# Attention of a hybrid block: order of the tensor engine's work within a unit

## The chip, the cores and the metric

The kernel runs on one core of a Trainium2 chip, one launch for both layers. The metric is the time of one execution on the device in microseconds (us), the median of three runs. A profile shows one execution, with every instruction of the engines: TensorE (PE, its weight loads PEld), VectorE (DVE), ScalarE (ACT), GpSimd (POOL) and the queue of SyncE that issues DMAs (SP).

## What is computed

Two layers over 512 latent tokens and 256 context tokens of width 1024. Each layer projects its input once and feeds three branches (attention, a state space scan, a convolution module); each branch is projected again, multiplied by a gate and summed. What matters here is the attention and the gated sum:

```python
def _attend(q, k, v):
    s = jnp.einsum('bkgqd,bksd->bkgqs', q, k).astype(jnp.float32) * ATTN_SCALE
    p = jax.nn.softmax(s, axis=-1).astype(v.dtype)
    return jnp.einsum('bkgqs,bksd->bkgqd', p, v)

def gated_merge(ua, us, uc, gm, w_br_attn, w_br_ssd, w_br_conv, b_gate, w_out):
    g = jax.nn.sigmoid(gm.reshape(gm.shape[:-1] + (N_BRANCH, D_MODEL)) + b_gate)
    y = (g[..., 0, :] * (ua @ w_br_attn) + g[..., 1, :] * (us @ w_br_ssd)
         + g[..., 2, :] * (uc @ w_br_conv))
    return y @ w_out
```

There are 8 query heads on 2 key heads, of width 64. Latent queries read all 768 keys, context queries the 256 context keys. The second layer computes no context queries.

## The kernel before

Large projections (`mm_cm_steps`, L175) are sums of three matmuls of split operands: `hh`/`hl` are the high and low parts of the input, `whi`/`wlo` those of a weight, which arrives by DMA as `raw` and is split by ACT (L156) and DVE (L157). A step yields after at least 1,024 columns of matmul, so that such work can be handed out in small portions.

Attention goes in **units**: one pair of heads `hp2` (4 pairs) by one block of 128 queries `qi`. The first layer has 24 units (16 of latent queries, 8 of context queries), the second 16, all latent. Between `man.__enter__()` and `man.__exit__()` the order of PE's instructions is the order of the code; the other engines' order is chosen at build time by a scheduler with a timing model, by priority and readiness (weight loads have high priority), and is fixed in the program. Each engine runs its own list strictly in order and waits on semaphores.

A latent unit consists of these parts:

- `scores` (tiles `ps_l`, two banks of 512 columns, and `ps_c`, one bank for both heads' 256 context keys): 4 + 4 matmuls; DVE takes three maxima (L988, L992) and joins them (L995). The banks come from the pool `pw`, which has three.
- `exps`, a generator: ACT reads the three banks with four exponentials and their sums (L1004, L1006), DVE inverts the sums (L1010), and ACT (L1012) and DVE (L1014) scale one head's `pe` each.
- `turn`, three times: four transposes of `pe` by PE into a bank `pt_p`, copied into `pth` by ACT (L1034) or, the second one, by DVE (L1032).
- `pv`: 24 matmuls of `pth` with the values into a bank `po_v`, each of 64 columns of the array, two side by side; ACT copies the result into `oa` (L1050).

`pt_p` and `po_v` share the pool `po1` of three banks with `pt_qk` (transposes of rotated queries and keys, run by `pipe.turn()`) and `ps_mod` (the next layer's modulation, first layer only). A bank is handed on when its last reader is done. `pth` tiles come from a pool of seven small tiles.

A context unit has one bank of scores, one `turn` and 8 value matmuls.

Between these parts the merge of the scan's branch is handed out: `wv = Weave(...)` runs the gate projection `ps_gm` (24 matmuls per 512 columns of output), the branch projection `ps_br` (12) and, in the first layer, `ps_mod`. Its total of columns is divided by a count of turns: 13 (`ATTN_SPARE`, 9 in the second layer) plus 8 for each latent unit and 7 for each context unit. `wv.fill(w)` hands out w turns' worth; `wv.finish()` hands out what is left. So a turn, here called a piece, is 247,808 / 197 = 1,258 columns in the first layer and 159,744 / 137 = 1,166 in the second.

The code runs the units in a pipeline of depth one: for unit u, first `scores` of unit u + 1, with a piece after each of its three banks; then u's three `turn`s, each followed by one step of u + 1's exponentials and a piece; a piece; u's values; a piece. After a pair's last unit, `oa` is multiplied by the gate (L1077) and stored (L1079). Behind the units, `ua` (high and low part of each pair's output) is built from `oa` by ACT (L1089) and DVE (L1090), and the attention branch's merge reads it (`ps_br<-ua`).

Of the kernel before, what the change touches and what calls it, by code (L numbers as in the profile page):

```python
# [9 lines left out]
F32 = mybir.dt.float32  # L10
F32R = mybir.dt.float32r
AF = mybir.ActivationFunctionType
ALU = mybir.AluOpType
AX = mybir.AxisListType

P = 128
# [5 lines left out]
NTT = NT // P  # L22
NLT = NL // P
# [24 lines left out]
ATTN_SPARE = (13, 9)  # L48
CTX_TURN = 1.75
# [8 lines left out]
def hybrid_kernel(ctx, tc, xT, cc, consts, rope, mod_params, params, fnw, w_mod, w_cm, w_q, w_kvd, w_z,  # L58
                  w_br, w_out, out):
    nc = tc.nc  # L60
    V, S, G, T = nc.vector, nc.scalar, nc.gpsimd, nc.tensor
# [5 lines left out]
    mid = ctx.enter_context(tc.tile_pool(name="mid", bufs=1))  # L67
    wk = ctx.enter_context(tc.tile_pool(name="wk", bufs=6))
    fl = ctx.enter_context(tc.tile_pool(name="fl", bufs=3))
# [16 lines left out]
    def fill(shape, name):  # L86
        return fl.tile(shape, F32, tag="F", name=name)
# [7 lines left out]
    def pot(name):  # L95
        return po1.tile([P, 512], F32, tag="po1", name=name)
# [7 lines left out]
    def tok(tt):  # L104
        return slice(tt * P, (tt + 1) * P)
# [77 lines left out]
    def run(steps):  # L183
        for _ in steps:
            pass
# [122 lines left out]
    o_dr = [dr.tile([P, NT], F32, name=f"odr{k}") for k in range(4)]  # L308
# [3 lines left out]
    ga_dr = [dr.tile([P, NT], F32, name=f"gadr{k}") for k in range(4)]  # L312
# [4 lines left out]
    for li in range(2):  # L317
# [3 lines left out]
        ntok = NL if last else NT  # L321
        ntt = ntok // P
# [3 lines left out]
        def rope_tables(cw, sw, o, eng):  # L326
# [5 lines left out]
            for hf in range(2):  # L332
                for b in range(2):
# [9 lines left out]
                        op0=ALU.mult)  # L343
# [18 lines left out]
        for k in range(0, KD, 2):  # L362
            if li == 0:
                for q in (4 + k // 2, k // 2):
                    wm = bigt([P, 2, KD, P], F32, "wm")
                    with tc.high_priority(offset=2 * TOP):
# [4 lines left out]
                                   in1=pmod[:, li, O_NW + k:O_NW + k + 2].unsqueeze(2).to_broadcast([P, 2, 2]),  # L371
                                   op0=ALU.add, op1=ALU.mult)
# [540 lines left out]
        for j in range(len(decays) + ahead):  # L913
            i = j // 2
# [54 lines left out]
        qts.append(bigt([P, 4, ntok], F32R, "qt"))  # L969
        later = [partial(q_prep, 1, t0) for t0 in range(0, ntt, 2)]  # L970

        def scores(hp2, qi, fill):

            g, hq = hp2 // 2, hp2 % 2 * 2
            lat = qi < NLT
            pl = [pwt("ps_l") for _ in range(2)] if lat else []
            pc2 = pwt("ps_c")
            mx = sm.tile([P, 2, 2], F32, tag="mx", name="mx", bufs=4)

            def qk(ps, j, a, b):  # L980
                for i in range(2):
                    T.matmul(ps[:, 0:b - a], qts[g][:, hq + j, tok(qi)], kk[:, i, g, a:b], start=(i == 0),  # L982
                             stop=(i == 1))

            if lat:
                for j in range(2):
                    qk(pl[j], j, 0, 512)
                    V.tensor_reduce(out=mx[:, 0, j:j + 1], in_=pl[j], axis=AX.X, op=ALU.max, negate=True)  # L988
                    fill()
            for j in range(2):  # L990
                qk(pc2[:, j * 256:(j + 1) * 256], j, 512, 768)
            V.tensor_reduce(out=mx[:, 1, :], in_=pc2.rearrange("p (j k) -> p j k", j=2), axis=AX.X, op=ALU.max,  # L992
                            negate=True)
            if lat:
                V.tensor_tensor(out=mx[:, 1, :], in0=mx[:, 0, :], in1=mx[:, 1, :], op=ALU.min)  # L995
            fill()
            sr = sm.tile([P, 2, 2], F32, tag="sr", name="sr", bufs=4)
            pes = [work([P, (NTT if lat else 2) * P], F32, "pe") for _ in range(2)]

            def exps():  # L1000
                for j in range(2):
                    bias, r = mx[:, 1, j:j + 1], sr[:, 1, j:j + 1]
                    if lat:
                        S.activation(pes[j][:, 0:512], pl[j], AF.Exp, bias=bias, accum_out=sr[:, 0, j:j + 1])  # L1004
                        yield
                    S.activation(pes[j][:, 512 if lat else 0:], pc2[:, j * 256:(j + 1) * 256], AF.Exp, bias=bias,  # L1006
                                 accum_out=r)
                    if lat:
                        V.tensor_tensor(out=r, in0=sr[:, 0, j:j + 1], in1=r, op=ALU.add)
                    V.reciprocal(r, r)  # L1010
                    if j == 0:
                        S.activation(pes[j], pes[j], AF.Copy, scale=r)  # L1012
                    else:
                        V.tensor_scalar(out=pes[j], in0=pes[j], scalar1=r, scalar2=None, op0=ALU.mult)  # L1014
                    yield

            return pes, exps()

        def values(hp2, qi, pes, oa, nexp, fill):
            g = hp2 // 2  # L1020
            k0, nk = (0, NTT) if qi < NLT else (NLT, NTT - NLT)
            po = pot("po_v")

            def turn(k1):
                pt = pot("pt_p")
                for i in range(2):
                    for j in range(2):
                        T.transpose(pt[:, tok(2 * i + j)], pes[j][:, tok(k1 + i)], ident)  # L1028
                pth = small([P, 2, 2, P], F32, "pth")
                pf = pth.rearrange("p k j q -> p (k j q)")  # L1030
                if k1 == 2:
                    V.tensor_copy(pf, pt)  # L1032
                else:
                    S.activation(pf, pt, AF.Copy)  # L1034
                next(nexp, None)
                fill()
                return pth

            def pv(k1, pth):
                for i in range(2):  # L1040
                    for j in range(2):
                        T.matmul(po[64 * j:64 * j + 64, 0:P], vv[:, k0 + k1 + i, g, :], pth[:, i, j, :],  # L1042
                                 start=(k1 + i == 0), stop=(k1 + i == nk - 1), tile_position=(0, 64 * j))

            pths = [turn(k1) for k1 in range(0, nk, 2)]
            run(nexp)
            fill()
            for k1, pth in zip(range(0, nk, 2), pths):
                pv(k1, pth)
            S.activation(oa[:, tok(qi)], po[:, 0:P], AF.Copy)  # L1050
            fill()


        units = [(hp2, qi) for hp2 in range(HEADS // 2) for qi in range(ntt)]
        while pipe.done < NTT // 2 + 1:
# [4 lines left out]
        wv = Weave(chain(merge_steps(1, us, False, False), ahead_steps(ahead0, ahead1)),  # L1060
                   merge_cols + (ahead1 - ahead0) * 24 * ntok,
                   ATTN_SPARE[li] + sum(8 if qi < NLT else 4 * CTX_TURN for _, qi in units))
        pes, exps = scores(*units[0], wv.fill)
        run(exps)
        for ui, (hp2, qi) in enumerate(units):
            cur = pes
            exps = iter(())
            pipe.turn()
            if ui + 1 < len(units):
                pes, exps = scores(*units[ui + 1], wv.fill)  # L1070
            if qi == 0:
                oa = mid.tile([P, ntok], F32, tag="H", name="oa", bufs=2)
            values(hp2, qi, cur, oa, exps, wv.fill if qi < NLT else partial(wv.fill, CTX_TURN))
            if qi == ntt - 1:
                gl = fl.tile([P, ntok], F32, tag="C", name="gl", bufs=1)
                nc.sync.dma_start(gl, ga_dr[hp2][:, :ntok])
                V.scalar_tensor_tensor(out=oa, in0=oa, scalar=0.5, in1=gl, op0=ALU.mult, op1=ALU.mult)  # L1077
                if hp2 < 3:
                    nc.sync.dma_start(o_dr[hp2][:, :ntok], oa)  # L1079
        wv.finish()  # L1080
        man.__exit__(None, None, None)

# [179 lines left out]
```

## Time and profile before

| | |
|---|---|
| median of 3 runs | 1495.2 us (1494.25 to 1498.19) |
| profiled execution: time of the run | 1495.54 us |
| profiled execution: span, first to last instruction | 1493.8 us |
| mean granted TensorE clock | 0.994 |
| attention of layer 1, from the first scores | about 520 to 718 us |
| attention of layer 2, from the first scores | about 1239 to 1383 us |

The page of a profile gives each engine's busy time and its share of the span; the rows below come from it and from views of the trace: sums over stretches of time ("windows"), who waited for whom ("waits"), and the instructions in order of time ("timeline"). Two neighbouring matmuls overlap in the records, since they are pipelined: the distance between their starts, not their duration, is what one costs.

### The profile page before, as it was taken

How to read it: one execution, taken by the hardware profiler on the slowest of the kernel's cores; microseconds unless marked ns; L12 is line 12 of the kernel's file. 1: busy time of each engine (PE TensorE's matmuls, PEld its weight loads, DVE VectorE, ACT ScalarE, POOL GpSimd, SP SyncE). 2: the span in 40 equal slices, each digit the busy share in tenths (PEclk: the TensorE clock that was granted, in tenths of full speed). 3: DMA queues.
4: the chain of work that ended last, by engine and by line, in shares of the span. 5: the costliest groups of instructions: out<-in, count | busy, mean ns of one | idle time of the engine just before them, and what ended most of it. 6: DMA issues, size and time to landing. Idle time of an engine off the chain costs nothing.

```text
span 1493.8 us, 25061 instructions
## 1 busy us (share of the span) xinstructions
PE 1450.1 (97%) x9716; PEld 1255.5 (84%) x9716; DVE 1039.1 (70%) x1911; ACT 721.9 (48%) x1624; POOL 81.6 (5%) x177
## 2 busy tenths in 40 slices
PE   5999999999999999999999989999999999999997
PEld 4889899988888888888888877989988887888886
DVE  4689998666568675555344377899977788666564
ACT  4423543364445475555333154355455557666341
POOL 0000010100002110000000000001010021000000
PEclk9999999999999999999999999999999999999998
DMA  9222333223233322323652532213423242322542
GB/s 377 69 72 94 108 117 111 76 71 103 100 114 123 124 94 99 121 64 121 226 176 92 173 114 86 82 57 110 152 78 106 96 151 78 105 85 91 185 141 78
DMA packets 69687, 172.58 MB, mean 116 GB/s; under 512 B 7872, under 2 KB 24384, under 8 KB 69568
## 3 DMA queue, kind: packets, MB, share of 16 engines
q1 hardware_dynamic: 69568, 170.98, 34.8%
q8 instruction: 76, 1.25, 0.3%
q14 instruction: 43, 0.35, 0.1%
HBM read 143.43 MB, written 27.53 MB: 114 GB/s over the span
## 4 chain that ended last, share of the span: by engine, by line
PE 91%; DMA 2%; DVE 2%; ACT 2%; issue 1%; SPq 0%; POOL 0%; POOLq 0%; DVEq 0%; ACTq 0%
PE ps_gm L175 23%; PE ps_br L175 11%; PE ps_xbc L175 9%; PE ps_o L175 6%; PE ps_gcv L175 4%; PE ps_g L175 4%; PE ps_u L175 4%; PE po_v L1042 3%; PE ps_ga L175 3%; PE pt_p L1028 3%; PE ps_l L982 2%; PE ps_mod L229 2%; PE ps_z L216 1%; PE ps_q L216 1%; PE ps_q L217 1%; PE ps_z L217 1%
## 5 line engine op out<-in xcount | busy, mean ns | idle before, releaser
L156 ACT ACTIVATE whi<-raw 128x512 fp32r<-128x512 f32 (+1 forms) x316 | 199.0, 632 | 280.8 <-PE ps_gm L175 63.8
L157 DVE TENSOR_TENSOR wlo<-raw,whi 128x512 fp32r<-128x512 f32 (+1 forms) x316 | 216.9, 690 | 148.0 <-ACT whi L156 144.0
L175 PE MATMUL ps_gm<-hh,whi 128*128 128x512 f32 (+1 forms) x576 | 212.6, 369 | 0.0
L408 DVE SCALAR_TENSOR_TENSOR vacc<-vt,par,vacc 128x783 f32<-128x783 f32 (+1 forms) x232 | 206.5, 890 | 8.1 <-ACT vacc L405 4.5
L175 PE MATMUL ps_gm<-hh,wlo 128*128 128x512 f32 (+1 forms) x576 | 210.1, 365 | 0.0
L175 PE MATMUL ps_gm<-hl,whi 128*128 128x512 f32 (+1 forms) x576 | 209.6, 364 | 0.0
L175 PEld LDWEIGHTS ps_gm<-hh,whi 128*128 128x128 f32 x576 | 109.0, 189 | 16.4 <-issue 3.1
L175 PEld LDWEIGHTS ps_gm<-hh,wlo 128*128 128x128 f32 x576 | 109.0, 189 | 15.1 <-issue 1.7
L175 PEld LDWEIGHTS ps_gm<-hl,whi 128*128 128x128 f32 x576 | 109.0, 189 | 13.8 <-issue 0.9
L175 PE MATMUL ps_xbc<-hh,whi 128*128 128x512 f32 (+1 forms) x240 | 83.0, 346 | 0.0
L175 PE MATMUL ps_xbc<-hh,wlo 128*128 128x512 f32 (+1 forms) x240 | 82.1, 342 | 0.0
L175 PE MATMUL ps_xbc<-hl,whi 128*128 128x512 f32 (+1 forms) x240 | 82.0, 342 | 0.0
L1034 ACT ACTIVATE pth<-pt_p 128x512 f32<-128x512 f32 x72 | 43.6, 605 | 55.8 <-PE pt_p L1028 55.7
L653 ACT ACTIVATE tg<-ps_gm,hw 128x512 f32<-128x512 f32 x72 | 44.2, 614 | 51.1 <-PE ps_gm L175 51.1
L175 PE MATMUL ps_o<-yh,whi 128*128 128x256 f32 (+1 forms) x208 | 65.8, 317 | 1.5 <-DVE xnew L1105 1.4
L175 PE MATMUL ps_o<-yl,whi 128*128 128x256 f32 (+1 forms) x208 | 65.7, 316 | 0.0
L175 PE MATMUL ps_o<-yh,wlo 128*128 128x256 f32 (+1 forms) x208 | 65.7, 316 | 0.0
L522 DVE SCALAR_TENSOR_TENSOR xacc<-xraw,par,xacc 128x770 f32<-128x770 f32 (+1 forms) x64 | 63.4, 999 | 3.0 <-ACT xacc L519 2.8
L682 DVE SCALAR_TENSOR_TENSOR tg<-tg,ps_br 128x512 f32<-128x512 f32 x66 | 39.6, 600 | 34.0 <-PE ps_br L175 30.5
L1028 PE MATMUL pt_p<-mr,pe 128*128 128x128 f32 x416 | 62.4, 272 | 0.0
L988 DVE TENSOR_REDUCE mx<-ps_l 128x1 f32<-128x512 f32 x64 | 44.1, 690 | 24.1 <-PE ps_l L982 23.4
L1028 PEld LDWEIGHTS pt_p<-mr,pe 128*128 128x128 f32 x416 | 50.9, 140 | 11.7 <-issue 0.2
(276 smaller groups left out, 3661.7 us busy)
## 6 DMA issues: line engine op xcount, KB each, us to landing
raw<-in_w_cm_dram SPq DMA_DIRECT2D x96, 512.0 KB, 3.6
raw<-in_w_mod_dram SPq DMA_DIRECT2D x32, 512.0 KB, 3.6
raw<-in_w_br_dram SPq DMA_DIRECT2D x24, 512.0 KB, 3.7
raw<-in_w_out_dram SPq DMA_DIRECT2D x21, 512.0 KB, 3.7
wm<-in_w_mod_dram SPq DMA_DIRECT2D x16, 512.0 KB, 9.2
ydr<-tg SPq DMA_DIRECT2D x16, 384.0 KB, 4.9
yo<-ydr SPq DMA_DIRECT2D x16, 384.0 KB, 3.8
raw<-in_w_z_dram SPq DMA_DIRECT2D x8, 512.0 KB, 3.9
```

The lines of the kernel that those rows point to most:

```text
L156: S.activation(hi, raw[:, u0:u0 + m, :], AF.Copy)
L157: V.tensor_tensor(out=lo, in0=raw[:, u0:u0 + m, :], in1=f(hi), op=ALU.subtract)
L175: T.matmul(ps[:, :b - a], st[:, col], mv(k)[:, a:b], start=(n == 0), stop=(n == len(order) - 1))
L216: T.matmul(ps[:, :ncol], xh(k)[:, t], hi, start=(k == 0), stop=False)
L408: V.scalar_tensor_tensor(out=acc[:, :n] if j else vt[:, o:o + n], in0=vt[:, o + j:o + j + n], scalar=cw(j), in1=acc[:, :n], op0=ALU.mult, ...
L522: xm = V.scalar_tensor_tensor(out=acc[:, :n], in0=raw[:, j:j + n], scalar=par[:, O_SCW + ct * 5 + j:O_SCW + ct * 5 + j + 1], in1=acc[:, :n ...
L653: lambda ps, a, b: S.activation(tg[:, a:b], ps, AF.Tanh, scale=0.5, bias=hw[:, br * 8 + ct:br * 8 + ct + 1]), "ps_gm")
L682: V.scalar_tensor_tensor(out=tg[:, a:b], in0=tg[:, a:b], scalar=1.0, in1=ps, op0=ALU.add, op1=ALU.mult)
L988: V.tensor_reduce(out=mx[:, 0, j:j + 1], in_=pl[j], axis=AX.X, op=ALU.max, negate=True)
L1028: T.transpose(pt[:, tok(2 * i + j)], pes[j][:, tok(k1 + i)], ident)
L1034: S.activation(pf, pt, AF.Copy)
L1042: T.matmul(po[64 * j:64 * j + 64, 0:P], vv[:, k0 + k1 + i, g, :], pth[:, i, j, :], start=(k1 + i == 0), stop=(k1 + i == nk - 1), tile_posi ...
```

## The change

The parts of a unit are put in another order on PE. For unit u: the eight score matmuls of unit u + 1 in one go; six pieces of the merge (a context unit: three of 1.75), after each of them but the last ones a step of the exponentials of u + 1; then, without a piece between, the values of unit u - 1 and all transposes of unit u; then two pieces (a context unit: one of 1.75). So the values run one unit later than before, the copies `pth` live on until then, and the gate of `oa` moves into `values`. Before the loop, the first unit's scores are followed by half of `ATTN_SPARE` in pieces (6.5 and 4.5); the last unit's values run after the loop, followed by what is left of the merge.

```diff
-        def scores(hp2, qi, fill):
+        def scores(hp2, qi):
...
                     V.tensor_reduce(out=mx[:, 0, j:j + 1], in_=pl[j], axis=AX.X, op=ALU.max, negate=True)
-                    fill()
...
                 V.tensor_tensor(out=mx[:, 1, :], in0=mx[:, 0, :], in1=mx[:, 1, :], op=ALU.min)
-            fill()
...
-        def values(hp2, qi, pes, oa, nexp, fill):
-            g = hp2 // 2
-            k0, nk = (0, NTT) if qi < NLT else (NLT, NTT - NLT)
-            po = pot("po_v")
-
-            def turn(k1):
+        def turned(hp2, qi, pes):
+
+            pths = []
+            for k1 in range(0, NTT if qi < NLT else NTT - NLT, 2):
                 pt = pot("pt_p")
...
-                next(nexp, None)
-                fill()
-                return pth
-
-            def pv(k1, pth):
-                for i in range(2):
-                    for j in range(2):
-                        T.matmul(po[64 * j:64 * j + 64, 0:P], vv[:, k0 + k1 + i, g, :], pth[:, i, j, :],
-                                 start=(k1 + i == 0), stop=(k1 + i == nk - 1), tile_position=(0, 64 * j))
-
-            pths = [turn(k1) for k1 in range(0, nk, 2)]
-            run(nexp)
-            fill()
-            for k1, pth in zip(range(0, nk, 2), pths):
-                pv(k1, pth)
+                pths.append(pth)
+            return pths
+
+        def values(hp2, qi, pths):
+            g, k0, nk = hp2 // 2, 0 if qi < NLT else NLT, 2 * len(pths)
+            po = pot("po_v")
+            for k in range(nk):
+                for j in range(2):
+                    T.matmul(po[64 * j:64 * j + 64, 0:P], vv[:, k0 + k, g, :], pths[k // 2][:, k % 2, j, :],
+                             start=(k == 0), stop=(k == nk - 1), tile_position=(0, 64 * j))
+            if qi == 0:
+                oas.append(mid.tile([P, ntok], F32, tag="H", name="oa", bufs=2))
+            oa = oas[-1]
             S.activation(oa[:, tok(qi)], po[:, 0:P], AF.Copy)
-            fill()
+            if qi == ntt - 1:
+                gl = fl.tile([P, ntok], F32, tag="C", name="gl", bufs=1)
+                nc.sync.dma_start(gl, ga_dr[hp2][:, :ntok])
+                V.scalar_tensor_tensor(out=oa, in0=oa, scalar=0.5, in1=gl, op0=ALU.mult, op1=ALU.mult)
+                if hp2 < 3:
+                    nc.sync.dma_start(o_dr[hp2][:, :ntok], oa)
...
-        pes, exps = scores(*units[0], wv.fill)
+        oas, before = [], None
+        pes, exps = scores(*units[0])
+        wv.fill(ATTN_SPARE[li] / 2)
         run(exps)
-        for ui, (hp2, qi) in enumerate(units):
+        for ui, unit in enumerate(units):
             cur = pes
             exps = iter(())
             pipe.turn()
             if ui + 1 < len(units):
-                pes, exps = scores(*units[ui + 1], wv.fill)
...
+                pes, exps = scores(*units[ui + 1])
+            lat = unit[1] < NLT
+            turns = 8 if lat else 4
+            for t in range(turns):
+                if t == turns * 3 // 4:
+                    run(exps)
+                    if before is not None:
+                        values(*before)
+                    before = (*unit, turned(*unit, cur))
+                next(exps, None)
+                wv.fill(1 if lat else CTX_TURN)
+        values(*before)
+        oa = oas[-1]
         wv.finish()
```

## Rows read from the trace of the kernel before

**Rows 1.** The page: busy time, share of the span and instructions of each engine.
```profile
PE 1450.1 (97%) x9716; PEld 1255.5 (84%) x9716; DVE 1039.1 (70%) x1911; ACT 721.9 (48%) x1624; POOL 81.6 (5%) x177
```

**Rows 2.** Windows: both attention stages; engines' busy us (instructions), granted clock, DMA.
```profile
520.00:718.00 198.00, 196.24 (x1593) 165.87 (x1592) 118.03 (x281) 122.25 (x319) 6.19 (x6) 1.00 0.33 106
1238.60:1383.00 144.40, 142.58 (x1022) 115.97 (x1023) 101.48 (x229) 95.27 (x240) 3.66 (x4) 0.99 0.26 86
```

**Rows 3.** Windows, the same columns: one latent unit of layer 2, transposes to transposes.
```profile
1311.39:1319.93 8.54, 8.54 (x63) 6.99 (x62) 7.11 (x16) 5.57 (x14) 0.00 (x0) 1.00 0.42 139
```

**Rows 4.** Waits of PE: line, waited for: us in total, times, longest.
```profile
PE ps_l L982 <- ACT pe L1004: 3.0, 2, 1.5
...
PE po_v L1042 <- ACT pth L1034: 0.2, 1, 0.2
```

**Rows 5.** Timeline at the head of layer 1's attention: start, us, instruction [idle before].
```profile
523.44 0.80 PE L857 MATMUL pt_qk<-mr,qhl 128*128 128x128 f32 x8
...
524.90 0.69 ACT L1004 ACTIVATE pe<-ps_l,mx 128x512 f32<-128x512 f32 x1
...
525.74 0.73 PE L982 MATMUL ps_l<-kk,qt 128*128 128x512 f32 x2 [1.50 <-ACT pe L1004]
```

**Rows 6.** Timeline of PE: transposes, then values, between pieces of the merge.
```profile
1304.65 0.60 PE L1028 MATMUL pt_p<-mr,pe 128*128 128x128 f32 x4
1305.00 0.48 PE L175 MATMUL ps_gm<-hh,wlo 128*128 128x512 f32 x1
1305.32 0.40 PE L175 MATMUL ps_gm<-hh,whi 128*128 128x512 f32 x1
1305.55 0.40 PE L175 MATMUL ps_gm<-hl,whi 128*128 128x512 f32 x1
...
1314.79 0.40 PE L175 MATMUL ps_gm<-hl,whi 128*128 128x512 f32 x1
1315.11 1.53 PE L1042 MATMUL po_v<-pth,vv 128*64 128x128 f32 x24
1316.58 0.50 PE L175 MATMUL ps_gm<-hh,wlo 128*128 128x512 f32 x1
1316.91 0.39 PE L175 MATMUL ps_gm<-hh,whi 128*128 128x512 f32 x1
```

**Rows 7.** Timeline of PE: transposes directly behind narrow matmuls.
```profile
548.50 0.65 PE L229 MATMUL ps_mod<-raw,sc 128*32 128x128 f32 x16
549.07 0.66 PE L1028 MATMUL pt_p<-mr,pe 128*128 128x128 f32 x4
...
549.80 0.39 PE L175 MATMUL ps_gm<-hl,whi 128*128 128x512 f32 x1
```

**Rows 8.** Timeline: ACT's copy of the values' bank, two units with and one without delay.
```profile
554.58 0.26 ACT L1050 ACTIVATE oa<-po_v 128x128 f32<-128x128 f32 x1
...
1316.69 0.28 ACT L1050 ACTIVATE oa<-po_v 128x128 f32<-128x128 f32 x1
...
1374.94 1.53 PE L1042 MATMUL po_v<-pth,vv 128*64 128x128 f32 x24
...
1376.03 0.97 ACT L1012 ACTIVATE pe<-pe,sr 128x768 f32<-128x768 f32 x1
1376.86 0.72 ACT L653 ACTIVATE tg<-ps_gm,hw 128x512 f32<-128x512 f32 x1
1377.43 0.31 ACT L1050 ACTIVATE oa<-po_v 128x128 f32<-128x128 f32 x1
```

**Rows 9.** Timeline behind layer 2's attention: first merge matmul of `ua`, last low part.
```profile
1392.94 0.62 PE L175 MATMUL ps_br<-ua,whi 128*128 128x512 f32 x2
...
1394.83 0.69 DVE L1090 TENSOR_TENSOR ua<-og,ua 128x512 fp32r<-128x512 f32 x1 [0.56 <-ACT ua L1089]
```

**Rows 10.** Windows, columns as in rows 2: a stretch of transposes and waits, and the next.
```profile
1235.90:1239.30 3.40, 2.35 (x18) 1.78 (x18) 2.73 (x7) 3.25 (x7) 1.05 (x1) 1.00 0.63 199
1239.30:1242.70 3.40, 3.40 (x10) 2.63 (x9) 2.31 (x6) 0.72 (x2) 0.00 (x0) 0.50 0.02 6
```

More of the change, by code (lines that the diff above doesn't have):

```diff
@@ L1069, in hybrid_kernel @@
             if ui + 1 < len(units):
-                pes, exps = scores(*units[ui + 1], wv.fill)
[L1071 to L1079, printed above, removed]
+                pes, exps = scores(*units[ui + 1])
[11 more added lines that the diff above has]
+        oa = oas[-1]
         wv.finish()
```

## Prediction

> **What bounds the kernel now.** I read the page first: PE is busy for 97% of the span, every other engine for at most 70% [rows 1]. A busy share alone says little, since matmuls overlap in the records, so the next question is whether PE ever stands still where the change works. The windows over the two attention stages answer it: PE is idle for 1.76 us of 198 and 1.82 us of 144.4 [rows 2], 3.6 us in all. The view of PE's waits names nearly all of that: twice 1.5 us in which the second unit's `ps_l` waits for the first unit's exponentials, and one 0.2 us wait of `po_v` [rows 4]. A latent unit in the middle of a stage has no idle time at all: 8.54 us, PE busy for 8.54 [rows 3]. So reordering can gain by three ways only: the 3.6 us of idle time, a cheaper passage from one kind of matmul to the next, and a higher clock. It can lose wherever a wait that a piece of the merge covers today is laid bare.
>
> **What a unit costs on PE, by starts.** Merge matmuls of 512 columns start every 0.23 us (1305.32, 1305.55) [rows 6]. Four transposes at 1304.65 put off the second matmul behind them to 1305.32: 0.67, less one matmul's 0.23, is 0.44, or 0.11 a transpose. For the values: from the merge matmul at 1314.79 to the second one behind at 1316.91 are 2.12 us, less two matmuls, 1.66; 12 pairs at 0.11 would be 1.32, so going into and out of the narrow matmuls costs 0.34. The transposes show no such price: four single ones cost as much as a run of them would. A piece is 1,166 columns x 0.23 / 512 = 0.52 us in the second layer and 1,258 columns, 0.57 us, in the first.
>
> **The change, part by part.**
>
> *Scores in one go.* Eight matmuls of the same kind as the merge's; splitting them cost nothing, joining them gains nothing. The three banks are needed at once and earlier: the next unit's scores start when the exponentials of the last must have read them. From the end of the scores to the next scores there were five pieces, transposes and values; now there are eight pieces, transposes and values, about 1.5 us more. No wait here inside the stage: 0.
>
> *6.5 or 4.5 pieces behind the first scores.* This is where both 1.5 us waits stand. In layer 1 PE goes from `pt_qk` at 523.44 (8 transposes) into a wait until 525.74, and the first exponential starts at 524.90 [rows 5]. Behind the first unit's last scores there was one piece so far; with 6.5 and 4.5 there are 5.5 and 3.5 more, 3.1 and 1.8 us of matmul in front of the second unit's scores. Both exceed the 1.5 us of wait, the second by little. I take both waits as gone: -3.0, and -0.2 for the values' wait on `pth`, which is now a unit old when it is read. Bounds: -3.2 and, if the waits move to the next bank, -1.5.
>
> *Values and transposes together.* The narrow matmuls are still entered from a merge matmul, but left into transposes. The trace has one neighbour of that: transposes directly behind `ps_mod`, also narrow [rows 7]. `ps_mod` ends at 549.15 (548.50 + 0.65), the second merge matmul behind the four transposes starts at 549.80, 0.65 later; behind `po_v`, ending at 1316.64, the second merge matmul comes at 1316.91, 0.27 later [rows 6]. Four transposes thus cost 0.38 there instead of 0.44: -0.06 a unit, and for 24 + 16 units -2.4. Bounds: 0 (the passage is no cheaper with `po_v`) and -0.17 a unit, half of the 0.34 if the way out cost nothing, -6.8.
>
> *The banks of `po1`.* A latent unit's group takes four banks out of three: `po_v`, then three `pt_p`. Pieces used to lie between; now the third set of transposes needs the bank of `po_v`, copied out by ACT. From rows 7, the first transposes start 0.08 before the end of the narrow ones, the first four take 0.41 (549.07, and a merge matmul that starts behind them), the second four 0.44: the third four are due 0.77 us after the values' end. An undelayed copy ends in time: `po_v` ends at 1316.64, `oa` runs from 1316.69 to 1316.97, 0.33 after [rows 6, 8]. But ACT works in order. In the last but one unit the values end at 1376.47, ACT still has a scaling of 0.97 and a gate of 0.72, and `oa` ends at 1377.74, 1.27 after: 0.50 too late [rows 8]. Of the 32 latent units, 12 have their copy end later than 0.77 after the values (the first starts at 554.58, the last at 1377.43 [rows 8]), and their excess adds up to 4.6 us. Today nothing waits for it. Does the change empty ACT's list in front of the copy? The values come six pieces behind the scores, 3.1 us, instead of five pieces and three sets of transposes, 3.9; the exponentials and the scaling hang on the scores and come no sooner. In that unit the scaling ended at 1377.00, 0.5 behind the values' end, and an earlier group only widens that. I therefore carry the 4.6 over. Bounds: 0, where the scheduler puts the copy first, and 0.5 in each of 32 units, +16.
>
> *Behind the attention.* `wv.finish()` covers 4.5 instead of 9 pieces, 2.4 us less in layer 2, while the chain from `oa` to the last low part of `ua` stays. There that part starts at 1394.83 and takes 0.69, while the merge of `ua` starts at 1392.94 [rows 9]: within the first tiles it comes just in time. The order is the scheduler's again there and it can put gate projections first: +0.5, bounds 0 and +2.4.
>
> *Nothing, or hidden:* the later store of `oa` (its reader comes behind the attention); DVE's three maxima in a row (2.1 us, then pieces of 3 us); six small tiles in place of three at the moment when old and new `pth` meet (of seven; the old three are read before the new ones are written).
>
> **The sum.** -3.0 - 0.2 - 2.4 + 4.6 + 0.5 = -0.5. The profiled execution took 1495.5 us with what lies around its span, 0.3 above the median; the forecast is 1495.0, no change. A measurement of this kernel can tell about 0.3%, 4.5 us, from no change: faster means below 1490.7, slower above 1499.7.
>
> **The rivals.**
>
> *The full gain.* If the copy of `po_v` comes first in ACT's list, the 4.6 us fall away: -5.6 to -5.1, 1490; with the passage out of narrow matmuls free, 1486. For it: 20 of 32 copies are in time today. Against: the change does nothing for the other 12. Chance 0.26.
>
> *Slower: the third transposes wait for the bank in most units.* Place: between the second and third `pt_p`. Price: the 0.5 us of the delayed rows in each of 32 units is +16, with -5.6 and +0.5 some 1506. It decides from a mean of (4.5 + 5.1) / 32 = 0.30 us a unit on. In the first layer `ps_mod` holds a third bank at times, which makes the second set wait too. Against: most copies are undelayed. Chance 0.16, of which 0.13 slower.
>
> *`ua` late.* +2.4 in layer 2 and, if layer 1's cover (13 to 6.5 pieces, 3.7 us) counts fully, 6.1 in all: about 1500.5. For it: rows 9. Against: layer 1 spends over 20 us between the stage and that merge. Chance 0.09, half of it slower.
>
> *The clock falls.* The group is 2.9 us in which PE runs transposes and narrow matmuls only. Once before in this stage PE passed a stretch with transposes and 1.05 us of idle time (busy 2.35 of 3.40), and the granted clock fell to 0.50, that is 1.2 of 2.4 GHz, for the next 3.4 us [rows 10], which costs 1.7 us. If one unit in four brought that on, 10 x 1.7 = +17: about 1507. Against: the group has no idle time. The Trainium skill, "TensorE: Matmul & The Clock Gate", section "Part 4: PE-mode transpose", says that transposes do not count as busy for the clock in the way matmuls do; by that rule this group would be the worst place of the kernel. The trace agrees only as far as rows 10 go, where idle time is mixed in. Chance 0.06, nearly all slower.
>
> The forecast itself, the waits of rows 8 carried over and a net change within 4.5 us, has 0.43.
>
> **The numbers.** Faster by over 0.3%: 0.23 of the full gain's 0.26. Slower: 0.13 + 0.04 + 0.05 = 0.22. The same: 0.55. For the range I go down to 1489.5, most of the full gain, and up to 1503, half way into the waiting bank; outside are the cheap passage, the clock and the worst of the bank, about 0.2. The forecast's own range is 1491 to 1499.
>
> **What would show it.** The two `ps_l` waits are gone from PE's waits; `pt_p` appears there, waiting for ACT `oa`, with 2 to 8 us in total; from `po_v` to the first transposes no gap, the group 2.9 us long; a unit without a wait takes 8.5 us. The prediction is wrong by its largest term if `pt_p` waits for nothing, or by 0.3 us and more a unit; it is wrong in kind if the granted clock drops in the middle of a stage, or if a row of the stage behind, `ps_br<-ua`, shows a wait of over 2 us.

## The result, and the profile after

The changed kernel takes 1506.3 us (median of 4 runs, 1504.32 to 1506.66) beside 1495.2 for the kernel before: ratio 1.0061, 95% interval 1.0044 to 1.0077. It is slower, by 11.1 us by the medians and by 9.1 (6.6 to 11.5) by the ratio. The forecast was 1495.0, no change, with a range up to 1503.0. The profiled execution took 1506.66 us (before: 1495.54, so 11.1 us less), its span is 1504.9, the mean granted clock 0.993; the readings below are made against these 11.1. Three executions of the kernel before that took 4770 to 8082 us, in one of the sets below, are left out of every number.

The page looks almost as before: PE is still busy for 97% of the span, as in [rows 1].

```profile
PE 1453.7 (97%) x9716; PEld 1258.0 (84%) x9716; DVE 1036.4 (69%) x1911; ACT 725.1 (48%) x1624; POOL 82.1 (5%) x177
```

The windows over the two attention stages of the changed kernel, from the first scores to a little past the last values (columns as in [rows 2]), already show more:

```profile
520.00:729.00 209.00, 204.51 (x1644) 175.08 (x1642) 121.17 (x287) 125.99 (x321) 5.92 (x6) 1.00 0.34 111
1242.50:1400.00 157.50, 152.24 (x1056) 123.64 (x1057) 100.53 (x231) 98.49 (x244) 3.67 (x4) 0.99 0.26 87
```

PE stands still for 4.49 and 5.26 us where it was 1.76 and 1.82 [rows 2]. The changed kernel's view of PE's waits says for whom:

```profile
PE pt_p L1024 <- ACT oa L1044: 6.6, 11, 1.8
...
PE pt_p L1024 <- DVE pth L1028: 1.6, 2, 0.8
...
PE ps_l L982 <- ACT pe L1002: 1.3, 3, 0.5
...
PE ps_br L175 <- ACT ua L1094: 0.6, 2, 0.4
...
PE ps_br L175 <- DVE ua L1095: 0.3, 1, 0.3
```

`pt_p` now waits eleven times for ACT's copy `oa` and twice for DVE's copy `pth` of the set before it; of the 3.0 us of `ps_l` [rows 4] 1.3 are left, and the merge of `ua` waits as well. Four latent units in the middle of layer 2's stage, values to values (windows of the changed kernel), are these, against 8.54 in [rows 3]:

```profile
1300.35:1308.80 8.45, 8.45 (x64) 7.09 (x63) 4.33 (x10) 4.64 (x12) 0.00 (x0) 1.00 0.27 86
1308.80:1318.13 9.33, 8.69 (x63) 7.07 (x62) 6.48 (x15) 6.36 (x15) 0.00 (x0) 1.00 0.26 88
1318.13:1326.81 8.68, 8.68 (x64) 7.08 (x63) 4.99 (x13) 5.55 (x16) 0.00 (x0) 1.00 0.29 94
1326.81:1336.13 9.32, 8.71 (x63) 7.07 (x63) 6.26 (x14) 5.17 (x13) 0.00 (x0) 1.00 0.27 87
```

A unit whose group goes through takes 8.45, less than before; two whose groups wait take 9.3 (the third, 8.68, has a stall of 0.15). The granted clock is 1.00 throughout. The timeline of one group that waits (changed kernel; PE's group first, then from the end of the next unit's scores on: DVE's joined maximum and ACT's list over the same stretch) shows the place:

```profile
1308.80 1.53 PE L1039 MATMUL po_v<-pth,vv 128*64 128x128 f32 x24
1310.26 1.09 PE L1024 MATMUL pt_p<-mr,pe 128*128 128x128 f32 x8
1311.99 0.66 PE L1024 MATMUL pt_p<-mr,pe 128*128 128x128 f32 x4 [0.64 <-ACT oa L1044]
...
1305.03 0.65 PE L982 MATMUL ps_c<-kk,qt 128*128 128x256 f32 x4
...
1307.30 0.16 DVE L994 TENSOR_TENSOR mx<-mx 128x2 f32<-128x2 f32 x1
...
1307.49 0.69 ACT L1002 ACTIVATE pe<-ps_l,mx 128x512 f32<-128x512 f32 x1 [2.78 <-DVE mx L994]
...
1309.29 0.48 ACT L1004 ACTIVATE pe<-ps_c,mx 128x256 f32<-128x256 f32 x1
...
1309.73 0.64 ACT L156 ACTIVATE whi<-raw 128x512 fp32r<-128x512 f32 x1
1310.25 0.70 ACT L653 ACTIVATE tg<-ps_gm,hw 128x512 f32<-128x512 f32 x1
1310.82 0.95 ACT L1010 ACTIVATE pe<-pe,sr 128x768 f32<-128x768 f32 x1
1311.65 0.29 ACT L1044 ACTIVATE oa<-po_v 128x128 f32<-128x128 f32 x1
```

The values end at 1310.33. The copy that frees their bank stands in ACT's list behind four exponentials, a weight conversion, a gate and a scaling, and ends at 1311.94; the third set of transposes starts 0.05 later. ACT itself had been idle for 2.78 us, waiting for the maxima of the next unit's scores; so it is not overloaded, its work comes too late.

The starts of all groups give the size. Inside a group transposes start 0.109 us apart; in 16 of the 32 latent units' groups the ninth one, the first of the third set, starts 0.26 to 2.06 us behind the eighth. What exceeds 0.109 there adds up to 5.5 us in layer 1 and 5.3 in layer 2: **10.8 us of stall**. The view of waits has 8.2 (6.6 + 1.6) for it; the difference is the overlap of neighbouring matmuls that is lost around each wait.

Two of the sixteen, both in layer 1 and 0.95 us each by starts, are not waits for the bank of `po_v`:

```profile
554.24 0.28 ACT L1044 ACTIVATE oa<-po_v 128x128 f32<-128x128 f32 x1
...
554.91 0.66 PE L1024 MATMUL pt_p<-mr,pe 128*128 128x128 f32 x4 [0.79 <-DVE pth L1028]
```

ACT's copy had ended at 554.52; the third set waited for DVE's copy of the second (554.17 to 554.86), so it had the second set's bank. Why it was given that one is not shown; in the run with the copy on DVE, below, both are gone too. The other fourteen, 8.9 of the 10.8 us, are as in the timeline above.

Where the rest of the 11.1 us stands: layer 1's head lost its wait of 1.5; layer 2's kept 1.5 in smaller parts (1.3 on `ps_l`, 0.2 on `ps_c`). The merge of `ua`, from its first matmul to its last, takes 77.0 us instead of 76.1 in layer 1 and 41.3 (from 1401.97) instead of 39.0 (from 1392.94 [rows 9]) in layer 2.

### The profile page after: what moved, and what is told of

It is laid out like the page before. It is cut to its first block, busy times and chain, and to the rows that moved or that the text cites. A ratio compares the mean times of both kernels' runs of the same rounds, so it can differ in the third digit from the quotient of the medians.

```text
span 1504.9 us, 25059 instructions
## 1 busy us (share of the span) xinstructions
PE 1453.7 (97%) x9716; PEld 1258.0 (84%) x9716; DVE 1036.4 (69%) x1911; ACT 725.1 (48%) x1624; POOL 82.1 (5%) x177
## 4 chain that ended last, share of the span: by engine, by line
PE 87%; ACT 5%; DVE 3%; DMA 3%; issue 2%; SPq 0%; POOL 0%; POOLq 0%; DVEq 0%; ACTq 0%
PE ps_gm L175 21%; PE ps_br L175 10%; PE ps_xbc L175 9%; PE ps_o L175 6%; PE ps_u L175 4%; PE ps_gcv L175 4%; PE ps_g L175 4%; PE ps_ga L175 3%; PE pt_p L1024 3%; PE po_v L1039 2%; PE ps_l L982 2%; PE ps_mod L229 2%; PE ps_z L216 1%; PE ps_q L217 1%; PE ps_q L216 1%
## 5 line engine op out<-in xcount | busy, mean ns | idle before, releaser
L175 PE MATMUL ps_gm<-hh,wlo 128*128 128x512 f32 (+1 forms) x576 | 206.9, 359 | 0.0
L1002 ACT ACTIVATE pe<-ps_l,mx 128x512 f32<-128x512 f32 x64 | 43.9, 686 | 50.6 <-DVE mx L994 50.6
L1024 PE MATMUL pt_p<-mr,pe 128*128 128x128 f32 x416 | 57.8, 280 | 8.2 <-ACT oa L1044 6.6
L1024 PEld LDWEIGHTS pt_p<-mr,pe 128*128 128x128 f32 x416 | 44.6, 141 | 18.8 <-ACT oa L1044 9.9
```

Of the source, the lines that this page charges most:

```text
L175: T.matmul(ps[:, :b - a], st[:, col], mv(k)[:, a:b], start=(n == 0), stop=(n == len(order) - 1))
```

## Experiments

Theory A: the third transposes wait for `po_v`'s bank, because its copy stands in ACT's list behind exponentials that come too late. Theory B: the group costs as such. Other losses (head, short cover for `ua`) were tried apart. Each run stood beside runs of the kernel before on the same chip, whose medians were 1496.1, 1494.7, 1498.4 and 1494.9 in the four sets (1495.2 beside the changed kernel); where a difference of times and one of ratios tell different stories, the text says so.

| kernel | us | ratio to before, 95% | stall in groups, us |
|---|---|---|---|
| the change | 1506.3 | 1.0061 [1.0044, 1.0077] | 10.8 |
| copy on DVE | 1497.4 | 1.0011 [1.0000, 1.0023] | 0.7 |
| before, copy on DVE | 1496.9 | 1.0008 [0.9997, 1.0019] | no group |
| scaling on DVE | 1499.0 | 1.0030 [1.0014, 1.0045] | 2.5 |
| group after 7 pieces | 1503.9 | 1.0060 [1.0044, 1.0076] | 5.4 |
| group after 5 pieces | 1511.1 | 1.0092 [1.0076, 1.0107] | 16.6 |
| piece inside the group | 1505.7 | 1.0064 [1.0048, 1.0080] | 4.8 |
| before, head only | 1496.1 | 1.0000 [0.9988, 1.0011] | no group |
| longer tail | 1502.4 | 1.0040 [1.0024, 1.0056] | 8.2 |
| copy on DVE, tail | 1495.0 | 0.9997 [0.9986, 1.0008] | 1.8 |
| copy on DVE, tail, head | 1493.9 | 0.9975 [0.9962, 0.9988] | 1.7 |
| the same again | 1493.0 | 0.9981 [0.9970, 0.9992] | 1.7 |
| the same, 7 pieces more tail | 1495.2 | 0.9984 [0.9971, 0.9997] | 1.8 |

**The copy of the bank on another engine** (`e1_copy_dve`).

```diff
-            S.activation(oa[:, tok(qi)], po[:, 0:P], AF.Copy)
+            V.tensor_copy(oa[:, tok(qi)], po[:, 0:P])
```

> The changed kernel with the copy of po_v into oa on DVE instead of ACT; all else the same. Theory A (the third transposes wait for po_v's bank because its copy stands behind exponentials, gate and scaling in ACT's list; the stalls inside the groups add up to 10.8 us): DVE has little in its list at that moment, the copy ends about 0.35 to 0.9 us after the values, the stalls in the groups fall below 3 us and the time to 1497 to 1500 us. Theory B (the loss lies elsewhere: in the passage from values to transposes, in the shorter cover behind the attention, in the order of other work): the time stays within 3 us of 1506.

Measured 1497.4: one line takes back 8.9 us by the medians, 7.5 by the ratios. In its view of waits no line says that `pt_p` waits for `oa`, or for DVE's `pth`; the largest for `pt_p` is the second of these, and the head's wait stays:

```profile
PE ps_l L982 <- ACT pe L1002: 1.3, 3, 0.5
...
PE pt_p L1024 <- ACT pth L1030: 0.2, 1, 0.2
```

The unit that waited in the changed kernel is here (windows) as short as one that goes through:

```profile
1302.02:1310.49 8.47, 8.47 (x63) 7.08 (x62) 6.67 (x16) 5.96 (x14) 0.00 (x0) 1.00 0.22 74
```

**Control: the same edit in the kernel before** (`e8_before_copy_dve`), where no `pt_p` needs that bank at once.

> The kernel before with the copy of po_v on DVE: the control. Nothing waits for the bank there, so by theory A nothing is gained: 1496.1, within 1.5 us. If the copy on DVE is a gain by itself (ACT relieved of 40 copies of 0.28 us), the kernel before gets faster as well, by several us, and the gain of that copy in the changed kernel says little of the bank.

Measured 1496.9, ratio 1.0008: nothing gained. PE has 1.6 us of new waits here (`po_v` for ACT's `pth` 1.0 instead of 0.2, `pt_p` for DVE's `pe` 0.8), which could hide a gain of that size, not one of 7.5. Relieving ACT of the copies is worth little or nothing by itself; what it is worth in the changed kernel is the stall.

**Another work of ACT taken from in front of the copy** (`e6_scale_dve`): the copy stays ACT's, the first head's scaling goes to DVE.

```diff
-                    if j == 0:
-                        S.activation(pes[j], pes[j], AF.Copy, scale=r)
-                    else:
-                        V.tensor_scalar(out=pes[j], in0=pes[j], scalar1=r, scalar2=None, op0=ALU.mult)
+                    V.tensor_scalar(out=pes[j], in0=pes[j], scalar1=r, scalar2=None, op0=ALU.mult)
```

> The changed kernel with the first head's scaling of the exponentials on DVE, like the second head's, instead of on ACT; the copy of po_v stays on ACT. Theory A (the third transposes wait for po_v's bank because the copy stands in ACT's list behind the late exponentials and the scaling): that scaling takes 0.95 us of ACT in front of the copy, and only one of the sixteen stalls is longer than that (1.95 us), so of the 10.8 us of stalls about 1 is left and the time comes to 1497, near the 1497.4 of the kernel with the copy on DVE; pt_p waiting for oa is nearly gone from PE's waits. Theory B (the stall belongs to the group itself, to the passage from values to transposes or to the bank being read while PE is next to it, and the copy on DVE won by being another engine's read): the copy is still ACT's, so the time stays within 2 us of 1506.3. Theory C (DVE, given 24 + 16 scalings more, becomes late with the second set's pth and the maxima): pt_p waits for DVE pth instead, 1500 to 1506.

Measured 1499.0, below the changed kernel by 7.3 us (4.6 by the ratios). The same unit's timeline in this kernel (PE, then ACT's list to the copy):

```profile
1304.03 1.53 PE L1036 MATMUL po_v<-pth,vv 128*64 128x128 f32 x24
1305.49 1.62 PE L1021 MATMUL pt_p<-mr,pe 128*128 128x128 f32 x12
...
1305.02 0.64 ACT L156 ACTIVATE whi<-raw 128x512 fp32r<-128x512 f32 x1
1305.54 0.70 ACT L653 ACTIVATE tg<-ps_gm,hw 128x512 f32<-128x512 f32 x1
1306.11 0.29 ACT L1041 ACTIVATE oa<-po_v 128x128 f32<-128x128 f32 x1
```

The list is the same without the scaling, and the copy ends 0.84 us after the values instead of 1.61. ACT still makes the copy and the group runs through in one. Theory B is out, and so is C: no `pt_p` waits for DVE's `pth`. The forecast was about 1 us of stall left and 1497; 2.5 were left (three groups), 1.5 of the 2 us by which it missed.

**The dose: the group one piece later and one earlier** (`e7_group_later`, `e11_group_earlier`).

```diff
-                if t == turns * 3 // 4:
+                if t == turns - 1:
```

> The changed kernel with the group of a latent unit behind seven of the eight pieces instead of six; context units as they are. Theory A: the exponentials get one piece, 0.52 us (0.57 in the first layer), of lead more; each of the sixteen stalls is shorter by so much, which leaves 1.4 + 0.4 + 0.4 + 0.2 + 0.2 in the first layer and about 1.0 in the second, 3.5 of 10.8 us: the time comes to 1499, at most 1501 as the next scores have a piece less in front of them. Theory B (the stall belongs to the group, wherever it stands): 1506.

```diff
-                if t == turns * 3 // 4:
+                if t == (5 if lat else 3):
```

> The changed kernel with the group of a latent unit behind five of the eight pieces instead of six (copy of po_v on ACT), the mirror image of the later group. Theory A (exponentials too close ahead of the group): every stall of the sixteen grows by one piece, 0.52 to 0.57 us, and some of the sixteen groups that went through now stall by up to as much: 10.8 + 8.7 = 19.5 us at least and 28 at most, so 1515 to 1523. Theory B (the stall belongs to the group, wherever it stands): 1506. If the scheduler moves ACT's other work, whi and tg, along with the pieces, so that less of it stands in front of the copy: about 1510.

Stalls behind 5, 6 and 7 pieces: 16.6, 10.8, 5.4 us, so 5.6 us for each piece that the exponentials are nearer to the group. That is theory A, and no stall that belongs to the group wherever it stands. My numbers were off for both, though. Of the earlier group I expected 19.5 us or more, 1515 at least, and got 16.6 and 1511.1: the stalls did not grow by the whole piece. That is the time of the third branch (about 1510), but not its reason: between the values' end and the copy, `whi` and `tg` take more of ACT than in the changed kernel, 5.8 us against 3.5 over all latent units. The time lies 4.8 above the changed kernel's; the stalls give 5.8, and the heads and `ua` wait 1.0 less. The later group should have come to 1499 and took 1503.9, a gain of 2.4 us by the medians and of none by the ratio, 1.0060. These lines of its waits say why:

```profile
PE ps_br L175 <- ACT ua L1094: 2.9, 1, 2.9
...
PE ps_l L982 <- ACT pe L1002: 2.6, 3, 1.4
...
PE pt_p L1024 <- ACT oa L1044: 1.8, 4, 0.7
```

Its stalls are shorter by 5.4, but the head of layer 2 waits 1.3 longer, and with only 10 merge matmuls between the last values and `ua` that waits 2.9 where it was 0.6 for the same line.

**A piece between values and transposes** (`e2_piece_between`): the bank gets 0.5 us more.

```diff
                         values(*before)
+                if t == (turns * 3 // 4 + 1 if lat else turns * 3 // 4):
                     before = (*unit, turned(*unit, cur))
```

> The changed kernel with one of the last two pieces of a latent unit moved in between its values and its transposes (context units as in the change). Theory A: every stall is covered by one piece, 0.52 to 0.57 us, longer; of the 10.8 us some 3.5 stay, so 1498 to 1500 us, and the merged group's cheaper passage (estimated 0.06 us a unit) is lost, +2 us: about 1500 to 1501. Theory B: within 3 us of 1506.

Measured 1505.7, a miss: I had 1500. Its waits:

```profile
PE ps_l L982 <- ACT pe L1002: 2.6, 3, 1.4
...
PE pt_p L1024 <- ACT oa L1044: 1.5, 2, 1.0
...
PE ps_br L175 <- ACT ua L1095: 1.4, 2, 1.0
...
PE ps_br L175 <- DVE ua L1096: 0.9, 1, 0.9
```

The stalls fell as they should, to 4.8 (-6.0). Against that, the passage is paid in full again: by starts, values between merge matmuls cost 1.66 and twelve transposes 1.31, 2.97 in all, where the group costs 2.92 (+1.6 over 32 units); `ps_l` waits 1.3 longer and `ua` 1.4 longer. That leaves -1.7; the profiled executions differ by -1.1. Here the granted clock also fell to 0.50 once at the head of layer 2's stage (1267.5 to 1270.9), behind those waits of `ps_l`. The parts add up after the fact; I had not counted them.

**The head alone, in the kernel before** (`e3_head_only`): scores of a stage's first unit without pieces between; their three pieces and half of the spare ones, which the end of the stage then lacks, behind them.

```diff
-        pes, exps = scores(*units[0], wv.fill)
+        pes, exps = scores(*units[0], lambda: None)
+        wv.fill(3 + ATTN_SPARE[li] / 2)
```

> The kernel before with the head of the change alone: the first unit's scores without pieces between, then three pieces plus half of the spare ones (9.5 and 7.5). Theory A: both waits of ps_l for the first exponentials, 1.5 us each, go: -3 us, 1492. Rival: the waits move to the next bank or the shorter cover behind the attention takes it back: within 1 us of 1495.

The two waits on `ps_l` are gone from its waits, and the time is not: ratio 1.0000. In their place are eight waits of `po_v` for ACT's `pth`, 2.1 us in all (one of 0.2 before), and one of `ua`, 1.2: 3.1 more for 3.0. The pieces put at the head are missing from the stage and its end; that they had been the cover there is the likely reading, not tried apart.

**A longer tail** (`e4_tail`): half of `ATTN_SPARE` more in the count of the weave, so that 13 and 9 pieces are left behind the stages.

```diff
-                   ATTN_SPARE[li] + sum(8 if qi < NLT else 4 * CTX_TURN for _, qi in units))
+                   1.5 * ATTN_SPARE[li] + sum(8 if qi < NLT else 4 * CTX_TURN for _, qi in units))
```

> The changed kernel with one and a half times the spare pieces, so that 13 and 9 of them are left behind the attention as before (the head keeps 6.5 and 4.5; a piece gets 3% smaller). Theory A: the merge of ua in layer 2, whose first 24 matmuls took 7.9 us instead of 5.5, starts late enough again: -2.4 us, 1504, while the stalls of the groups stay at about 10.8 us or grow by up to 0.5 us. Theory B (the 2.4 us are caused by something other than the cover): 1506 within 1 us.

Measured 1502.4, 3.9 less than the changed kernel. 2.6 of that are shorter stalls, which I had expected to stay; why they fell is not shown. The merge of `ua` took 40.5 us instead of 41.3 in layer 2 and 76.0 instead of 77.0 in layer 1. With both edits, copy and tail (`e5_copy_dve_tail`), the stall no longer clouds this:

> The changed kernel with the copy of po_v on DVE and half of ATTN_SPARE more in the weave's count, so that 13 and 9 pieces are left behind the stages as in the kernel before. The copy alone gave 1497.4, the tail alone took 3.9 us off the changed kernel, of which 2.6 were shorter stalls (8.2 us instead of 10.8) that the copy on DVE has already taken; 1.3 us is left for the tail. Theory A and a late ua as the second loss: 1496.1, between 1494.5 and 1497.4. If the tail is worth its whole 3.9 us: 1493.5, under the kernel before.

Measured 1495.0, ratio 0.9997 against 1.0011 with the copy alone: 2 us, the same order as the 1.3 expected, but the two intervals overlap.

**The head on top of both** (`e9_head`, and once more as `e12_head_again`).

```diff
-        wv.fill(ATTN_SPARE[li] / 2)
+        wv.fill(3 + ATTN_SPARE[li] / 2)
```

with 3 more in the count of the weave.

> The changed kernel with the copy of po_v on DVE, half of ATTN_SPARE more in the weave's count (tail of 9 pieces in the second layer) and three pieces more behind the first scores (9.5 and 7.5 instead of 6.5 and 4.5; the count is raised by 3 as well). Against the same kernel without the three pieces (1495.0): the 1.4 us in which ps_l waits for the exponentials at the head of the second layer's stage go, 3 pieces being 1.6 us. If that is what is left of the forecast's 3.0 us: 1493.6. If the wait moves on to the next bank or to ua, as it did in the kernel before with the same edit: 1495.

> The kernel with the longer head once more (copy of po_v on DVE, three pieces more at the head, half of ATTN_SPARE more behind), beside runs of the kernel before on one chip, because its ratio of 0.9975 came beside a kernel before that took 1498.8 there and 1494.7 to 1496.1 elsewhere. If the order of the change is a gain once its stalls are gone (both attention stages up to ps_o were 1.5 and 2.1 us shorter in the profile than in the kernel before): 0.9975 again, between 0.996 and 0.9985. If the ratio came from the kernel before on that chip: 0.999 to 1.000.

1493.9 and 1493.0, ratios 0.9975 and 0.9981 on two chips: both intervals end below 1. `ps_l` no longer waits for exponentials, and of the groups' waits these are left (first of the two runs):

```profile
PE pt_p L1024 <- ACT pth L1030: 0.7, 3, 0.3
...
PE pt_p L1024 <- DVE oa L1044: 0.3, 1, 0.3
```

This order, with the bank copied in time and the head and tail filled, is 0.2% faster than the kernel before (2.8 to 3.7 us), and the best seen here. The kernel before with the three edits together was not run, so how much of this belongs to the order alone is open.

**Still more tail** (`e10_head_tail`): 10 instead of 3 in that count.

> As the kernel with the longer head, with seven pieces more in the weave's count, so that about as many merge matmuls stand between the last values and the first ua as in the kernel before (45 in the second layer; 19 in the changed kernel, 29 with half of ATTN_SPARE more). The phase of ua in the second layer took 40.5 us with 29 and 41.3 with 19, 39.0 with 45. Theory that the short tail is the second loss: 1.4 us less than the kernel with the longer head in the second layer, nothing in the first: 1492.2, faster than the kernel before by 0.2 to 0.3 per cent. Rival (the pieces, 7 per cent smaller, bring the exponentials nearer to the group and pt_p waits again): 1494 to 1497.

1495.2 (1490.8 to 1499.3). The merge of `ua` in layer 2 fell from 41.1 to 39.6 as theory said, yet the time did not fall. The rival's time came, but not its reason: the stalls are 1.8 us, as without the seven pieces. In the profiled execution, the slowest of its twelve, `ps_mod` waits 0.7 and `pt_qk` 0.6 us for ACT's `pth`, which they did not in the run without the seven pieces. The granted clock dropped once at the head of layer 2, as it did in one of the two profiles without them. Whether more tail is worth anything stays open.

## Why the prediction was wrong

**The step that failed is the size of the bank's term: +4.6 forecast, 10.8 measured.** Place, releaser and mechanism were as written for fourteen of the sixteen stalls: the third set of transposes, ACT's copy `oa`, the list in order. The prediction took the lateness of twelve copies (ten of latent units, 3.1 us, and two of context units, 1.5, whose bank stands in front of a latent unit's transposes in the new order; not twelve of the 32 latent ones, as it says) as it stood in the old order, and noted, without a number, that an earlier group "only widens that". It had the number: values six pieces behind the scores, 3.1 us, instead of 3.9, so 0.8 us nearer. Added to each of the twelve late copies it gives 4.6 + 9.6 = 14; the dose runs, 5.6 us for 0.52, give 8.6 more at 0.8. Both are rough and too high, but either would have carried the forecast to 1500 and beyond. Sixteen groups stalled, not twelve.

It also wrote that the exponentials "come no sooner", and put DVE's three maxima in a row at nothing. They come later. In the timeline of the group above, the scores end at 1305.68 and the joined maximum at 1307.46, 1.78 behind; the same unit before:

```profile
1310.46 0.63 PE L982 MATMUL ps_c<-kk,qt 128*128 128x256 f32 x4
...
1312.12 0.16 DVE L995 TENSOR_TENSOR mx<-mx 128x2 f32<-128x2 f32 x1
```

1.19 behind. The medians over the latent units of layer 2 are 1.2 before and 1.8 after (layer 1: 1.3 and 1.7), and the last exponential ends 3.7 and 4.4 us behind the scores (4.1 and 4.3), while the values start 0.85 us sooner behind them in both layers. So the group came sooner and the exponentials in front of the copy came later; how much of the 10.8 is due to the later maxima was not tried apart.

**The rival "the third transposes wait in most units" was the case**, at its price (1506 against 1506.3) though not in most units: 16 of 32, at 0.68 on average instead of 0.50 in each. The mean, 10.8 / 32 = 0.34, lies above its deciding 0.30 (by the view of waits it is 8.2 / 32 = 0.26, below it). It had a chance of 0.16; with either estimate above it would have had the largest. That the times agree is luck: its parts were 16 for the bank and -5.1 for all else, the runs show 10.8 and about 0.

**Head: -3.0 forecast, -1.5 measured**, the prediction's own bound for waits that move to the next bank. Layer 1's wait went, layer 2's stayed: 4.5 pieces exceeded the wait "by little", and the first unit's exponentials had not read the second bank in time. One row of the changed kernel shows it:

```profile
1250.20 0.73 PE L982 MATMUL ps_l<-kk,qt 128*128 128x512 f32 x2 [0.50 <-ACT pe L1002]
```

7.5 pieces covered it (the run with the longer head).

**Passage: -2.4 forecast, about -1.9 by starts.** From the last merge matmul ahead to the second behind, less two of 0.233, a latent unit's values and transposes cost 3 x 0.436 + 1.66 = 2.97 before and 2.92 in groups without a stall, such as this one:

```profile
1300.02 0.40 PE L175 MATMUL ps_gm<-hl,whi 128*128 128x512 f32 x1
...
1301.81 1.53 PE L1024 MATMUL pt_p<-mr,pe 128*128 128x128 f32 x12
...
1303.41 0.39 PE L175 MATMUL ps_gm<-hh,whi 128*128 128x512 f32 x1
```

That is -0.05 a unit, and about as much in context units (1.22 before, 1.175 after). The wait of `po_v`, -0.2, went as well.

**`ua`: +0.5 forecast, +2.3 in layer 2 and +0.9 in layer 1 measured**, between the forecast and the rival "`ua` late". In the changed kernel, the first merge matmul of `ua` comes 4.7 us after the last values, before it was 10.7: 20 merge matmuls stood between instead of 46. The kernel before first (to be read with [rows 9]), then the changed kernel's last values and the first tiles of `ua`:

```profile
1380.69 1.53 PE L1042 MATMUL po_v<-pth,vv 128*64 128x128 f32 x24
...
1389.73 1.09 PE L1024 MATMUL pt_p<-mr,pe 128*128 128x128 f32 x8
1390.58 0.48 PE L175 MATMUL ps_gm<-hh,whi 128*128 128x512 f32 x1
...
1393.47 0.60 PE L1024 MATMUL pt_p<-mr,pe 128*128 128x128 f32 x4
...
1396.62 0.66 PE L1039 MATMUL po_v<-pth,vv 128*64 128x128 f32 x8
...
1401.97 0.76 PE L175 MATMUL ps_br<-ua,whi 128*128 128x512 f32 x2
...
1403.14 0.50 PE L175 MATMUL ps_br<-ua,whi 128*128 128x512 f32 x1 [0.18 <-ACT ua L1094]
1403.95 0.50 PE L175 MATMUL ps_br<-ua,whi 128*128 128x512 f32 x1 [0.31 <-DVE ua L1095]
```

The shorter tail, 4.5 pieces or 10 matmuls less, accounts for part of it only: with 30 matmuls between, the merge still took 40.5. Another part stands in the rows above: 12 gate projections lie between the second and the third set of the last unit's transposes and 2 more inside its values, where the code has the group in one. So at the end of this stage PE's order is not that of the code, against what was said of the whole stage ahead of the prediction, and the last values come some 3 us later by that work. The prediction had named the scheduler's order as a risk, but for work behind the values.

Together: -1.5 - 0.2 - 1.9 + 10.8 + 3.2 = 10.4 of the 11.1 us by which the two profiled executions differ. Behind each stall the tenth transpose also starts 0.165 us after the ninth instead of 0.109, 0.9 us over sixteen; with it the sum is 11.3.

**The rival "full gain" (1490)** did not come either when the stall was taken away: the copy on DVE gave 1497.4. The passage's 1.9 and the head's 1.5 stood against the 3.2 of `ua`. **The rival "clock"** was wrong: the granted clock was 1.00 in the stretches with groups, waiting or not. Its price, 1507, also left out the bank's term: 17 on top of the forecast of 1495.0 is 1512. The rule of the Trainium skill, "TensorE: Matmul & The Clock Gate", "Part 4: PE-mode transpose", by which this group would be the worst place of the kernel, did not show: no drop followed any of the groups of the changed kernel. A group holds 24 narrow matmuls besides its 12 transposes, so no run here tries transposes alone.

## What to carry to other kernels

When steps that share a ring of buffers are put back to back, the last one is due when the first one's buffer is free, and that is set by the list of the engine that frees it. Read the end of that copy against the new due time in every unit, and shift both by what the reordering itself shifts; a lateness that costs nothing today is not a bound. Then ask which work of the freeing engine must stand in front of the copy: moving the copy to DVE was one line and brought 7.5 to 8.9 us.

Pieces of cover have owners: moved to the head, they were missing behind the stage. Count matmuls between the last producer and the first consumer, before and after.

## Not expected of the hardware

A wait of PE costs more than the view of waits says. The one of 0.64 above moved the ninth transpose from 0.109 to 0.913 us behind the eighth, 0.80; over all groups 8.2 us of waits were 10.8 by starts, 0.16 more for each of sixteen.

The clock fell behind some stretches with waits and not behind others. In the run with the group later, `ua`'s wait of 2.93 us was followed by 0.50 of full clock, 1.2 of 2.4 GHz, for 3.4 us, and by full speed after (windows, columns as in [rows 2]):

```profile
1396.30:1399.70 3.40, 0.49 (x1) 0.19 (x1) 1.97 (x4) 2.09 (x4) 0.00 (x0) 1.00 0.80 310
1399.70:1403.10 3.40, 3.32 (x8) 2.66 (x9) 0.74 (x3) 1.32 (x2) 0.00 (x0) 0.50 0.48 154
```

In the changed kernel, the group with the longest stall was not followed by any drop, though PE was busy for only 2.21 of 4 us there:

```profile
540.00:544.00 4.00, 2.21 (x28) 1.80 (x25) 3.13 (x9) 4.00 (x12) 1.95 (x2) 1.00 0.01 2
544.00:548.00 4.00, 4.00 (x42) 3.42 (x41) 4.00 (x10) 2.13 (x5) 0.00 (x0) 1.00 0.34 100
```

So whether a stall brings the drop can't be read from its length in these rows alone.
